# A hybrid attention block on one core: where the rotary blocks stand in the queues, and where the head norms stand in TensorE's order

## The chip, the cores and the metric

The kernel runs on one core of one Trainium2 chip. The metric is the device time of one execution in microseconds (us), lower is better; the times below are medians over runs of the same program. A core has TensorE (matmuls; PE in the profile, PEld for its weight loads), VectorE (DVE), ScalarE (ACT), GpSimd (POOL) and SyncE (SP), which in this kernel issues all DMA transfers. Every engine takes its instructions from its own queue in order; an instruction that waits holds up all that stand behind it on the same engine.

## The reference

The input is x, 512 positions by 2048 features, float32. One layer:

- h = RMSNorm(x) times a gain; one projection of h with `w_in` (2048 x 10752) gives all columns: q, k, v and gate z of branch A, q, k, v and gate z of branch B, and two merge gates of 2048.
- Branch A is differential attention with 8 heads: q and k get a rotary embedding, two softmaxes p1 - lambda p2 are applied to v, and the result of each head is RMS-normalised over its 128 features.
- Branch B has 8 query heads and 2 key/value heads. Each head's q and k are RMS-normalised over 128 features, multiplied by a gain, and rotated by a 2-D ("axial") rotary embedding; then softmax attention.
- Each branch's result times SiLU(z) goes through its own output projection (1024 x 2048); the two are merged with sigmoid gates, projected once more (`w_o`, 2048 x 2048), added to x, and normalised with a final gain.

## The kernel before

All matmuls are done in a split form: a float32 matrix becomes a high part (a rounded copy, `w_hi`, made by ScalarE, line 111) and a low part (the rest, `w_lo`, made by VectorE, line 112), and each product is the sum of three matmuls. So a weight tile passes SP (load), ScalarE (high part), VectorE (low part) and then TensorE. Three buffers hold the split tiles (`wp`, line 90), so the splitting engines run at most a little ahead of TensorE.

Most of the projection is done in Strassen groups (`strassen`, line 193, and `strassen_wide`): a block of 512 columns is made from seven products, a11, a12, s1, s2, s3, s4 and a22, instead of eight. The sums and differences of the weight blocks that Strassen needs are further VectorE work (`sub`, line 214; "L216" in the profile). Each product is 48 matmuls over two weight tiles. When results are complete the group calls `done`, which adds (VectorE) and stores.

The work in order:

1. x is normalised and transposed; the first columns, one plain Strassen group and two wide groups give branch B's and part of branch A's columns, which go to the DRAM buffer `pv`, one block of 128 columns each.
2. Twelve Strassen groups make the gates za, zb, ga, gb (lines 636 to 650). `gate` adds the last product (line 641), applies SiLU or sigmoid on ScalarE (line 642) and stores (line 644). After each of the first ten groups the program text calls `rope_b(n)`, which handles one of branch B's ten blocks (8 query, 2 key): it reads the block from `pv` into a tile `cols` (line 595, two buffers), takes four sums of squares on ScalarE (line 599), turns them into factors on POOL (`rsqrt_pool`, lines 107 and 108), makes the rotary products on VectorE (two half products, line 610, then lines 611 and 612), for key blocks multiplies by the factor on ScalarE (line 615), and stores the block back to `pv` (line 616).
3. The attention stage (from line 940). TensorE's order is written out by hand there (`manual_schedule`): sixteen heads of both branches, in the order of `HEADS`, are woven with "filler" steps, pieces of the remaining projections of 12 or 24 matmuls. `fill(n)` issues n filler steps; `FILLS` holds three digits per head, f[0] to f[2], used at three places of the head's turn. In head n's turn `last.finish()` ends the previous head, and `last.norm()` does the RMS norm of the previous head if it was of branch A (lines 809 to 824; two matmuls with a matrix of 1/128, then Ln, Exp and Square on ScalarE, three operations on VectorE, one on POOL, and the split of the result, `og0h` and `og0l`, or its store). For a B head `norm` does nothing.
4. Output projections, merge, final projection with Strassen groups, residual and final norm.

Outside the hand-written part a planner sets the order of each engine's instructions: it goes through the program with modelled durations and puts an instruction into the queue when its inputs are ready by that model, earlier text first. So an instruction whose inputs are ready early can stand in the queue far ahead of its place in the text. `tc.keep_in_program_order(ins)` adds an order edge: `ins` stands behind the instruction that was traced just before it on the same engine. It adds no wait on the chip by itself.

Of the kernel before, what the change touches and what calls it, by code (L numbers as in the profile page):

```python
# [13 lines left out]
AF = mybir.ActivationFunctionType  # L14
ALU = mybir.AluOpType
# [36 lines left out]
def hybrid_block_kernel(  # L52
# [8 lines left out]
    nc = tc.nc  # L61
# [7 lines left out]
    def new_banks(unit):  # L69
        ps_pools.close()  # L70
        banks["pool"] = unit, ps_pools.enter_context(
            tc.tile_pool(name="ps_" + unit, bufs=1, space=bass.MemoryType.PSUM))

    def share_banks(**kw):
        banks.update(kw)
# [29 lines left out]
    def rsqrt_pool(dst, ss, mul, add, n):  # L105

        nc.gpsimd.tensor_scalar(out=dst, in0=ss, scalar1=mul, scalar2=add, op0=ALU.mult, op1=ALU.add)
        nc.gpsimd.tensor_tensor(out=dst, in0=dst, in1=neg_half[:, :n], op=ALU.pow)
# [322 lines left out]
    with tc.tile_pool(name="xs", bufs=1) as xs:  # L431
# [4 lines left out]
        sq = xs.tile([P, D], F32, name="sq", tag="s4h")  # L436
        with tc.tile_pool(name="xn", bufs=1) as xn:
# [16 lines left out]
            for t in range(NT):  # L454
                ss = xn.tile([P, 2], F32, name="ss", tag="ss", bufs=4)
# [6 lines left out]
                for c in (slice(0, 512), slice(512, 1024)):  # L462
                    v = xt[:, t].rearrange("p (k c) -> p k c", k=2)[:, :, c]
# [95 lines left out]
        with tc.tile_pool(name="sp", bufs=6) as sp:  # L559
            new_banks("bank")  # L560
            free = [2 * i + j for i in banks["acc"] for j in range(2)]
            share_banks(acc=free[:4])

            def tmp():
                return sp.tile([P, 2, 256], F32, name="kept", tag="kept")

            for blocks in STRASSEN_BLOCKS[1:]:
                project(blocks, tmp, lambda ps: tmp())

            tabs = {}  # L570

            def b_table(nm, src):

                g = sp.tile([P, P], F32, name="g_" + nm, tag="g_" + nm, bufs=1)
                nc.sync.dma_start(out=g, in_=src.broadcast_to([P, P]))
                tcb = sp.tile([P, NT, P], F32, name=f"tc_{nm}", tag=f"tc_{nm}", bufs=1)
                tsb = sp.tile([P, NT, P], F32, name=f"ts_{nm}", tag=f"ts_{nm}", bufs=1)
                nc.sync.dma_start(out=tcb, in_=cos_b.rearrange("(t p) c -> p t c", p=P))
                nc.sync.dma_start(out=tsb, in_=sin_b.rearrange("(t p) c -> p t c", p=P))
                gv = g.rearrange("p (h r j) -> p h r j", h=2, r=2)  # L580
                for t in range(NT):
                    nc.gpsimd.tensor_tensor(out=tcb[:, t, :], in0=tcb[:, t, :], in1=g, op=ALU.mult)
                    ov = tsb[:, t, :].rearrange("p (h r j) -> p h r j", h=2, r=2)
                    for r in range(2):
                        nc.gpsimd.tensor_tensor(out=ov[:, :, r, :], in0=ov[:, :, r, :],
                                                in1=gv[:, :, 1 - r, :], op=ALU.mult)
                tabs[nm] = tcb, tsb

            def rope_b(n):


                b = B_QB + n if n < 8 else B_KB + n - 8
                assert written[b] == NT
                v = sp.tile([P, NT, P], F32, name="cols", tag="cols", bufs=2)
                nc.sync.dma_start(out=v, in_=pv[b])
                sq = sp.tile([P, P], F32, name="bsq", tag="bsq", bufs=1)
                ss = rb[:, n, :]
                for t in range(NT):
                    nc.scalar.activation(out=sq, in_=v[:, t, :], func=AF.Square, accum_out=ss[:, t:t + 1])
                if n < 8:  # L600

                    rsqrt_pool(ss, ss, 1.0, P * EPS, NT)
                else:
                    rsqrt_pool(ss, ss, 1.0 / P, EPS, NT)
                t2 = sp.tile([P, NT, P], F32, name="rope2", tag="rope2", bufs=1)
                tcb, tsb = tabs["q" if n < 8 else "k"]
                for r in range(2):
                    d, s, m = (x.rearrange("p t (a r j) -> p t a r j", r=2, j=32)[:, :, :, q, :]
                               for x, q in ((t2, r), (v, 1 - r), (tsb, r)))
                    nc.vector.tensor_tensor(out=d, in0=s, in1=m, op=ALU.mult)  # L610
                nc.vector.tensor_tensor(out=v, in0=v, in1=tcb, op=ALU.mult)
                nc.vector.tensor_tensor(out=v, in0=v, in1=t2, op=ALU.add)
                if n >= 8:
                    for t in range(NT):
                        nc.scalar.mul(out=v[:, t, :], in_=v[:, t, :], mul=ss[:, t:t + 1])
                nc.sync.dma_start(out=pv[b], in_=v)

            b_table("q", q_norm_g)
            b_table("k", k_norm_g)
            to_rope = [0, 8, 1, 2, 3, 4, 5, 9, 6, 7]  # L620


            nc.sync.dma_start(out=sub_g, in_=subln_g.rearrange("o p -> p o"))
            nc.vector.tensor_scalar(out=sub_g, in0=sub_g, scalar1=LAM_INIT - 1.0, scalar2=None, op0=ALU.mult)
            lam4, lprod = (sp.tile([P, n, 64], F32, name="lam", tag="kept") for n in (4, 2))
            for i, v in enumerate((lq1, lk1, lq2, lk2)):
                nc.sync.dma_start(out=lam4[:, i, :], in_=v.broadcast_to([P, 64]))
            for i in range(2):
                nc.vector.tensor_tensor(out=lprod[:, i, :], in0=lam4[:, 2 * i, :], in1=lam4[:, 2 * i + 1, :], op=ALU.mult)
            nc.vector.tensor_reduce(out=lsum, in_=lprod, axis=AX.X, op=ALU.add)  # L630
            nc.scalar.activation(out=lsum, in_=lsum, func=AF.Exp)
            nc.vector.tensor_tensor(out=nlam, in0=lsum[:, 1:2], in1=lsum[:, 0:1], op=ALU.subtract)
            nc.vector.tensor_scalar(out=nlam, in0=nlam, scalar1=-LAM_INIT, scalar2=None, op0=ALU.add)


            for c0, n, func, dst in ((O_ZA, BW, AF.Silu, zg[0:BW]), (O_ZB, BW, AF.Silu, zg[BW:]),
                                     (O_GA, D, AF.Sigmoid, gg[0:D]), (O_GB, D, AF.Sigmoid, gg[D:])):
                for g in range(0, n, S):
                    def gate(th, ch, ps, sb, g=g, func=func, dst=dst):
                        v = tmp()  # L640
                        nc.vector.tensor_tensor(out=v, in0=ps, in1=sb, op=ALU.add)
                        nc.scalar.activation(out=v, in_=v, func=func)
                        row = g + ch * 256
                        nc.sync.dma_start(
                            out=dst[row:row + 256, th * 256:th * 256 + 256].rearrange("(c p) t -> p c t", p=P),
                            in_=v)

                    strassen(w_in, c0 + g, c0 + g + 256, xq, False, tmp, gate)
                    if to_rope:
                        rope_b(to_rope.pop(0))  # L650
# [284 lines left out]
    def fill(n):  # L935
        for _ in range(n):
            next(filler, None)


    with tc.manual_schedule(engines={mybir.EngineType.PE}):  # L940
        heads = [(HeadA if h[0] == "A" else HeadB)(int(h[1])) for h in HEADS]
        heads[0].prepare()
        heads[1].prepare()
        heads[0].double()
        fill(FILL_FIRST)
        heads[0].turn()
        fill(2)
        for n, head in enumerate(heads):
            f = [int(c) for c in FILLS[n]]
            last = heads[n - 1] if n else None  # L950
            if n + 1 < len(heads):
                heads[n + 1].double()
            head.scores(0)
            head.scores(1)
            fill(f[0])
            if last:
                last.finish()
            head.scores(2)
            head.scores(3)
            if n + 1 < len(heads):  # L960
                heads[n + 1].turn()
            if n + 2 < len(heads):
                heads[n + 2].prepare()
            fill(1)
            if last:
                last.norm()
            fill(f[1] - 1)
            head.turn_p()
            fill(f[2])
        head.finish()  # L970
        head.norm()
# [11 lines left out]
    for n, e in (("s3", "h"), ("s4", "l")):  # L983
        m = xa.tile([P, 2, 8, 256], F32R, name="m" + n, tag="a2" + e)
        mq[n] = m[:, 0], m[:, 1]
    with tc.tile_pool(name="ya", bufs=1) as yp:
# [5 lines left out]
        for n in range(4):  # L992
# [15 lines left out]
            s = yp.tile([P, 2, 256], F32, name="ms", tag="ms")  # L1008
# [196 lines left out]
```

## Time and profile before

| | us |
|---|---|
| median of three timed runs | 1376.71 |
| lowest and highest of them | 1376.68, 1381.0 |
| the profiled execution, its own time | 1378.97 |
| its span in the trace | 1377.2 |
| TensorE busy | 1341.6 (97%) |
| VectorE busy | 1083.4 (79%) |
| ScalarE busy | 707.6 (51%) |
| POOL busy | 168.0 (12%) |

How to read it: the span is the time from the first to the last instruction of one execution; busy times are shares of it. Matmuls overlap each other, so a busy TensorE isn't TensorE at its best, and progress is better read from how many matmuls start in a stretch. The gates' stage lies from about 265 to 760 us of the span, the attention stage from 760 to about 1120 us.

### The profile page before, as it was taken

The page shows a single profiled execution, that of the slowest core. Times are in us where ns is not written, and L with a number is a line of the kernel's source. Part 1 is how long each engine was busy: PE and PEld are TensorE (multiplying, and loading weights), DVE is VectorE, ACT ScalarE, POOL GpSimd, SP SyncE. Part 2 cuts the span into 40 slices and gives each one's busy share as a digit, 9 for nine tenths or more (in the row PEclk, how much of TensorE's full clock was granted, in tenths as well). Part 3 has the DMA queues.
Part 4 walks back from the last instruction along what each step waited for, and adds up shares of the span by engine and source line. Part 5 has one row for each costly group of instructions (what it writes and reads, how often), then busy time and mean ns, then how long its engine had stood idle before and what let it go on. Part 6 is the DMA issues. An engine that isn't in the chain of part 4 may idle for free.

```text
span 1377.2 us, 22754 instructions
## 1 busy us (share of the span) xinstructions
PE 1341.6 (97%) x8905; PEld 1234.5 (90%) x8905; DVE 1083.4 (79%) x1339; ACT 707.6 (51%) x1119; POOL 168.0 (12%) x154
## 2 busy tenths in 40 slices
PE   6999999999999999999999999999899999999997
PEld 6998888899899999999999888888688888899997
DVE  5976978789887777778776477877899958899886
ACT  7643333355544444444444476666777843354444
POOL 1000000063100000000000321330321000004322
PEclk9999999999999999999999999999999999999999
DMA  8244663575444543343455774554765446463333
GB/s 290 77 144 134 190 200 99 170 213 167 138 129 141 153 145 118 117 125 118 146 154 146 229 220 132 153 153 133 209 179 168 147 152 203 148 245 117 95 97 123
DMA packets 198893, 214.12 MB, mean 155 GB/s; under 512 B 11760, under 2 KB 159488, under 8 KB 198144
## 3 DMA queue, kind: packets, MB, share of 16 engines
q1 hardware_dynamic: 198784, 212.65, 49.7%
q8 instruction: 70, 1.15, 0.4%
q14 instruction: 39, 0.32, 0.1%
HBM read 172.76 MB, written 35.65 MB: 151 GB/s over the span
## 4 chain that ended last, share of the span: by engine, by line
PE 62%; DVE 7%; DMA 3%; ACT 3%; issue 3%; POOL 1%; SPq 0%; DVEq 0%; POOLq 0%; ACTq 0%
PE acc L241 36%; PE acc L182 19%; PE aux L744 3%; DVE w_lo L112 2%; PE aux L731 2%; PE aux L857 1%; DMA pv<-cols 1%; DVE w_raw L216 1%; DMA cols<-pv 1%; PE aux L787 1%; PE aux L788 1%; ACT w_hi L111 1%; DVE nmax L699 1%; DMA rows<-yg 0%; DVE pl L112 0%
## 5 line engine op out<-in xcount | busy, mean ns | idle before, releaser
L111 ACT CAST w_hi<-w_raw 128x1024 fp32r<-128x1024 f32 x357 | 374.3, 1050 | 481.4 <-PE acc L241 291.6
L112 DVE TENSOR_TENSOR w_lo<-w_raw,w_hi 128x1024 fp32r<-128x1024 f32 x357 | 445.3, 1250 | 166.2 <-ACT w_hi L111 164.8
L216 DVE TENSOR_TENSOR w_raw<-w_raw 128x1024 f32<-128x1024 f32 x136 | 171.0, 1258 | 1.8
L241 PE MATMUL acc<-a2h,w_lo 128*128 128x256 f32 x384 | 109.1, 284 | 1.9 <-DVE w_lo L112 1.9
L241 PE MATMUL acc<-a2h,w_hi 128*128 128x256 f32 x384 | 108.9, 284 | 0.0
L241 PE MATMUL acc<-a2l,w_hi 128*128 128x256 f32 x384 | 108.8, 283 | 0.0
L687 POOL TENSOR_TENSOR cols<-cols,ca 128x512 f32<-128x512 f32 x16 | 21.5, 1341 | 537.1 <-DMA other<-pv 412.1
L241 PEld LDWEIGHTS acc<-a2h,w_lo 128*128 128x128 f32 x384 | 73.8, 192 | 2.5 <-DVE w_lo L112 2.5
L241 PEld LDWEIGHTS acc<-a2h,w_hi 128*128 128x128 f32 x384 | 73.8, 192 | 0.3 <-ACT w_hi L111 0.3
L241 PEld LDWEIGHTS acc<-a2l,w_hi 128*128 128x128 f32 x384 | 73.8, 192 | 0.0
L699 DVE TENSOR_REDUCE nmax<-aux 128x1 f32<-128x512 f32 x96 | 61.5, 682 | 2.8 <-PE aux L788 2.8
L182 PE MATMUL acc<-a1h,w_hi 128*128 128x512 f32 (+1 forms) x160 | 57.6, 364 | 0.2 <-ACT a1h L485 0.2
L182 PE MATMUL acc<-a1h,w_lo 128*128 128x512 f32 (+1 forms) x160 | 56.9, 360 | 0.0
L182 PE MATMUL acc<-a1l,w_hi 128*128 128x512 f32 (+1 forms) x160 | 56.7, 360 | 0.1
L241 PE MATMUL acc<-s2h,w_lo 128*128 128x256 f32 x192 | 54.8, 286 | 2.0 <-DVE w_lo L112 2.0
L241 PE MATMUL acc<-a1h,w_hi 128*128 128x256 f32 x192 | 54.6, 284 | 1.8 <-DVE wide_u L330 1.6
L241 PE MATMUL acc<-s4h,w_lo 128*128 128x256 f32 x192 | 54.6, 285 | 1.1 <-DVE w_lo L112 1.1
L182 PE MATMUL acc<-a2h,w_hi 128*128 128x512 f32 (+1 forms) x160 | 55.6, 351 | 0.0
L182 PE MATMUL acc<-a2l,w_hi 128*128 128x512 f32 (+1 forms) x160 | 55.6, 348 | 0.0
L182 PE MATMUL acc<-a2h,w_lo 128*128 128x512 f32 (+1 forms) x160 | 55.4, 347 | 0.0
L241 PE MATMUL acc<-a1h,w_lo 128*128 128x256 f32 x192 | 54.6, 284 | 0.8 <-DVE w_lo L112 0.8
L241 PE MATMUL acc<-s1h,w_lo 128*128 128x256 f32 x192 | 54.5, 284 | 0.2 <-DVE w_lo L112 0.2
(353 smaller groups left out, 4218.0 us busy)
## 6 DMA issues: line engine op xcount, KB each, us to landing
w_raw<-in_w_in_dram SPq DMA_DIRECT2D x144, 512.0 KB, 3.9
w_raw<-in_w_in_dram SPq DMA_DIRECT2D x64, 256.0 KB, 4.0
w_raw<-in_w_o_dram SPq DMA_DIRECT2D x32, 512.0 KB, 4.0
cols<-pv SPq DMA_DIRECT2D x36, 256.0 KB, 3.5
gg<-kept SPq DMA_DIRECT2D x32, 256.0 KB, 2.5
w_raw<-in_w_out_b_dram SPq DMA_DIRECT2D x32, 256.0 KB, 3.8
rows<-gg SPq DMA_DIRECT2D x32, 256.0 KB, 3.4
w_raw<-in_w_out_a_dram SPq DMA_DIRECT2D x32, 256.0 KB, 3.3
```

The source lines that it names most:

```text
L111: nc.scalar.copy(out=hi, in_=src)
L112: nc.vector.tensor_tensor(out=lo, in0=src, in1=hi.bitcast(F32), op=ALU.subtract)
L182: nc.tensor.matmul(out=acc[b][:, place], lhsT=l, rhs=r, start=first and kc == order[0] and k == 0 and i == 0, stop=last and kc == order[-1 ...
L216: nc.vector.tensor_tensor(out=d, in0=u, in1=v, op=ALU.subtract)
L241: nc.tensor.matmul(out=ps[u] if by_row else ps[:, u, :], lhsT=l, rhs=r, start=n % (2 if by_row else 4) == 0 and k == 0 and i == 0, stop=n ...
L687: nc.gpsimd.tensor_tensor(out=v, in0=v, in1=ca, op=ALU.mult)
L699: nc.vector.tensor_reduce(out=nmax, in_=sps, axis=AX.X, op=ALU.max, negate=True)
L731: nc.tensor.transpose(out=tp[:, i * P:(i + 1) * P], in_=self.p[i][:, j * P:(j + 1) * P], identity=ident)
L744: nc.tensor.matmul(out=o, lhsT=l, rhs=r, start=j == 0 and i == 0, stop=j == NT - 1 and i == 2)
L787: nc.tensor.matmul(out=sp, lhsT=qs[:, sl], rhs=kh, start=True, stop=False)
L788: nc.tensor.matmul(out=sp, lhsT=qs[:, sl], rhs=kl, start=False, stop=True)
L857: nc.tensor.matmul(out=sp, lhsT=l, rhs=r, start=n == 0, stop=n == 2)
```

## The change

Two things are changed. In `rope_b`, the four squares on ScalarE and the two half products on VectorE are each kept behind the instruction traced before them on their engine: the first of them behind the last result of the Strassen group that the text has just before, the others behind each other. In the heads' loop, the previous head's norm changes place with filler steps: it stood behind one filler step and ahead of f[1] - 1 of them, and now stands behind f[1] - 1 and ahead of one.

```diff
                 for t in range(NT):
-                    nc.scalar.activation(out=sq, in_=v[:, t, :], func=AF.Square, accum_out=ss[:, t:t + 1])
+                    tc.keep_in_program_order(
+                        nc.scalar.activation(out=sq, in_=v[:, t, :], func=AF.Square, accum_out=ss[:, t:t + 1]))
...
-                    nc.vector.tensor_tensor(out=d, in0=s, in1=m, op=ALU.mult)
+                    tc.keep_in_program_order(nc.vector.tensor_tensor(out=d, in0=s, in1=m, op=ALU.mult))
...
-            fill(1)
+            fill(f[1] - 1)
             if last:
                 last.norm()
-            fill(f[1] - 1)
+            fill(1)
             head.turn_p()
```

## Rows read from the trace of the kernel before

**Rows 1.** The page, part 1: busy us, share of the span, instructions.
```profile
PE 1341.6 (97%) x8905; PEld 1234.5 (90%) x8905; DVE 1083.4 (79%) x1339; ACT 707.6 (51%) x1119; POOL 168.0 (12%) x154
```

**Rows 2.** Busy time of two equal stretches: stretch, length, each engine, clock, DMA.
```profile
283.00:374.00 91.00, 84.63 (x678) 81.84 (x677) 81.40 (x104) 52.52 (x127) 31.05 (x32) 1.00 0.55 171
374.00:465.00 91.00, 91.00 (x760) 91.00 (x759) 68.85 (x66) 39.70 (x43) 0.00 (x0) 1.00 0.46 143
```

**Rows 3.** The same columns (PE, PEld, DVE, ACT, POOL), operations on `cols` alone.
```profile
283.00:374.00 91.00, 0.00 (x0) 0.00 (x0) 22.05 (x40) 17.43 (x84) 0.00 (x0) 1.00 0.55 171
```

**Rows 4.** Waits, 283 to 374 us: who waited for whom, us, times, longest.
```profile
ACT bsq L599 <- DMA cols<-pv: 16.2, 7, 4.7
PEld acc L241 <- DVE w_lo L112: 8.1, 10, 1.3
DVE rope L610 <- DMA cols<-pv: 4.6, 3, 1.8
ACT cols L615 <- POOL rb L108: 3.5, 1, 3.5
```

**Rows 5.** Timeline of VectorE: start, us, what, count [idle before it, releaser].
```profile
298.38 0.76 DVE L610 TENSOR_TENSOR rope<-cols,ts_q 128x256 f32<-128x256 f32 x2 [1.72 <-DMA cols<-pv]
299.06 1.22 DVE L112 TENSOR_TENSOR w_lo<-w_raw,w_hi 128x1024 fp32r<-128x1024 f32 x1
```

**Rows 6.** Timeline of VectorE and TensorE around 280 to 287 us.
```profile
280.09 0.23 DVE L629 TENSOR_TENSOR lam<-lam 128x64 f32<-128x64 f32 x1 [2.47 <-DMA lam<-in_lambda_k_dram]
...
286.89 0.39 PE L241 MATMUL acc<-s2h,w_lo 128*128 128x256 f32 x1 [0.57 <-DVE w_lo L112]
```

**Rows 7.** Timelines of VectorE, ScalarE and weight loads at a group's end.
```profile
437.04 0.68 DVE L641 TENSOR_TENSOR kept<-acc,kept 128x512 f32<-128x512 f32 x1
...
438.77 1.22 DVE L112 TENSOR_TENSOR w_lo<-w_raw,w_hi 128x1024 fp32r<-128x1024 f32 x1
...
437.88 0.62 ACT L642 ACTIVATE kept<-kept 128x512 f32<-128x512 f32 x1
439.81 1.05 ACT L111 CAST w_hi<-w_raw 128x1024 fp32r<-128x1024 f32 x1 [1.30 <-issue]
...
442.68 0.19 PEld L241 LDWEIGHTS acc<-a2h,w_lo 128*128 128x128 f32 x1
```

**Rows 8.** Waits of SP's queue, 260 to 380 us, then 380 to 760 us.
```profile
SPq L595 <- DMA pv<-cols: 15.2, 8, 3.9
...
SPq L644 <- ACT kept L642: 188.1, 38, 12.5
```

**Rows 9.** Operations on `cols`: ns min/median/max, first and last start; POOL's timeline.
```profile
L610 DVE TENSOR_TENSOR rope<-cols,ts_q x16: 418/422/543, 286.8 to 364.4; 128x256 f32<-128x256 f32 x16
...
328.39 3.45 POOL L107 TENSOR_SCALAR rb<-rb 128x4 f32<-128x4 f32 x1 [6.70 <-ACT bsq L599]
```

**Rows 10.** Timeline of TensorE at the norm of head A1.
```profile
897.72 0.50 PE L813 MATMUL aux<-sql,ones 128*128 128x512 f32 x1 [0.88 <-DVE sql L112]
```

**Rows 11.** TensorE at the norm of head A2, and the stretch behind it.
```profile
973.48 0.50 PE L812 MATMUL aux<-sqh,ones 128*128 128x512 f32 x1 [0.96 <-ACT sqh L111]
976.29 0.80 PE L813 MATMUL aux<-sql,ones 128*128 128x512 f32 x1 [2.32 <-DVE sql L112]
...
977.00:982.00 5.00, 5.00 (x14) 3.81 (x13) 2.43 (x6) 3.22 (x8) 0.00 (x0) 0.52 0.89 256
```

**Rows 12.** Norms of A3 and A4: timelines, waits from 1000 to 1116 us, busy time.
```profile
1024.33 0.39 PE L812 MATMUL aux<-sqh,ones 128*128 128x512 f32 x1
...
1028.22 0.69 ACT L815 ACTIVATE y<-aux,eps_t 128x512 f32<-128x512 f32 x1
...
1039.09 0.62 ACT L111 CAST og0h<-rows 128x512 fp32r<-128x512 f32 x1 [3.07 <-POOL rows L823]
...
ACT og0h L111 <- POOL rows L823: 6.6, 4, 3.1
...
1040.00:1056.00 16.00, 15.91 (x70) 12.48 (x69) 15.68 (x31) 14.48 (x31) 0.00 (x0) 1.00 0.46 137
```

## The prediction

> **What bounds the kernel now.** I read the page first. TensorE is busy 1341.6 us of 1377.2 [rows 1], so only its gaps and slow stretches, some 35 us with the start and the end, can be won back, and any idle time of another engine counts only where it ends in one. The second view is the busy time by stretch. The two stretches of 91 us in [rows 2] are the same code from about the same place of a Strassen group of the gates, once of the first group and once of the third. In 374 to 465 us TensorE starts 760 matmuls and never idles: one each 91/760 = 0.120 us. In 283 to 374 us it starts 678, so 82 x 0.120 = 9.8 us went. VectorE is busy 81.4 us of 91 in that stretch against 68.9 us, and 22.05 us of the 81.4 are operations on `cols`, the rotary blocks [rows 3]. All ten blocks lie here, the half products between 286.8 and 364.4 us [rows 9]; later stretches have none. The third view is the waits of the stretch [rows 4]: weight loads wait 8.1 us, ten times, for `w_lo`, the low half of the weight split, which VectorE makes; and VectorE and ScalarE themselves stand 4.6 and 16.2 us at a rotary block whose read from DRAM has not landed. [rows 5] shows one case: VectorE idles 1.72 us for `cols`, does the two half products, and only then makes, at 299.06 us, the `w_lo` for which a weight load stands (the longest of those ten waits, 1.3 us). Both engines take their instructions in order, so a block that is early in the queue and late in its data stops the weight split behind it.
>
> **The rotary blocks.** Nothing is removed or added: 40 squares on ScalarE, 20 half products and 20 full products and sums on VectorE, 20 small POOL operations and the rest stay. What changes is their place. The first square and the first half product of block n are ordered behind the last SiLU/sigmoid and the last add of group n; the others follow by data or by the chained edges. So the blocks go from ten in 91 us to one per group, and a group is 336 matmuls x 0.120 = 40.3 us.
>
> *What goes.* The 9.8 us, less what the blocks didn't cause. Just before, VectorE stood 2.47 us for the lambda vectors, and the `w_lo` that came behind them made TensorE wait 0.57 us at 286.89 us [rows 6]. The stretch lost 9.8 us of starts for 91 - 84.63 = 6.4 us of idle time, because the matmuls behind a gap start slower, so a gap costs 1.54 times its length: 0.9 us stay. Gain 9.8 - 0.9 = 8.9 us. The two reads that are issued at the start land long before their group ends; the other eight follow the store of the block two before, so they have about a group (40 us) where now they have none. The 4.6 and 16.2 us of waits go, and nothing of that kind is late next.
>
> *What a block costs in its new place.* On VectorE 22.05/10 = 2.2 us in one piece behind the last add; on ScalarE 17.43/10 = 1.75 us [rows 3], four squares with their accumulator reads. [rows 7] is such a place in the steady part: the add at 437.04 us, a subtraction, then the split that ends at 438.77 + 1.22 = 439.99 us, whose weights TensorE loads at 442.68 us. The lead is 2.7 us. With 2.2 us put behind the add, 0.5 us is left; the next ScalarE cast starts at 439.81 us, and the squares (from 438.5 us, 1.75 us long) delay it by 0.4 us, which the 2.2 us on VectorE hide. The two products that follow, a11 and a12, need no subtraction, so VectorE makes a split in 1.22 us for each tile of 24 matmuls, 2.88 us, and recovers 1.6 us a tile. I take 0 per group. If the lead were as short as inside 283 to 374 us, each block would cost its whole 2.2 us (22 us in ten groups); if the planner uses the room better, nothing is gained beyond the 9.8 us. The place read at 437 us is nearest, hence 0, with up to 0.6 us a group (6 us) kept for the range. The two key blocks also hold ScalarE for four multiplications that wait for POOL, 3.5 us in the one case seen [rows 4]; against the 2.7 us lead that is at most 0.8 us each, 1.6 us for the range.
>
> *Queues.* SP gets a store and a read per block; the read waits for a store to land, 15.2 us in eight, at most 3.9 [rows 8]. In the steady part SP stands 188.1 of 380 us for gate results, up to 12.5 us at a time [rows 8], so the block's store and read fit into such a pause: cost 0. If that cover were gone, the weight loads queued behind would start up to 3.9 us later in each of eight groups; how much of it TensorE would see I can't read, at most 31 us, at least 0, and the pauses put it at 0. POOL is empty from 374 to 760 us [rows 2], and nobody waits for its query factors before the heads.
>
> A rule speaks against the bursts. Row first: while POOL's little factor operation on 128x4 ran beside VectorE's two-input products, it took up to 3.45 us, but the half products had a median of 0.422 us and a longest of 0.543, against a shortest of 0.418 [rows 9]: POOL paid, hardly VectorE. The Trainium skill, GPSIMD Engine Reference, section 1 Specifications, says that POOL's SBUF interfaces are shared with VectorE, with contention for VectorE instructions that have two SBUF inputs; every operation of the burst is one. If VectorE paid, a burst could double to 4.4 us and pass the lead by 1.7 us, 17 us in ten groups; by this trace's row the sum stays.
>
> **The norms.** `fill(1)` and `fill(f[1] - 1)` swap places around `last.norm()`. Norm work exists only after an A head. With a middle digit of 2 (the heads after A0 and A2) both are 1 and nothing moves. It moves for A1 and A3 to A6, by one filler step, 12 matmuls x 0.227 = 2.7 us later; A7's stands outside the loop. A1's second norm matmul waits 0.88 us for `sql` [rows 10]; 2.7 us later `sql` is there, so 0.9 us go. A3 to A6 had practically no wait (TensorE is busy 15.91 of 16 us around A4's [rows 12]): 0 to 0.4 us, I take 0. The norm's chain (Ln, Exp, Square, three on VectorE, the product on POOL) starts up to 2.7 us later; its tiles are next needed by the `finish` of the A head behind, nearly a whole head later. A2's stall, the largest of the attention part, stays: 0.96 and 2.32 us of waits, and then 5 us at a granted clock of 0.52, the 1.2 GHz level for nearly all of that stretch, which is 5 x 0.48 = 2.4 us lost [rows 11].
>
> **Sum.** -8.9 (blocks) + 0 (bursts) - 0.9 (A1) + 0 (other norms) = -9.8 us. The profiled execution took 1378.97 us (1377.2 us of span and 1.8 around it), so it would be 1369.2 us. Against the median of the three timed runs, 1376.71 us, which is 2.3 us lower, it is 1366.9 us; I say 1367.
>
> **Rivals.**
> *A: the bursts cost.* The order in VectorE's queue is planned with modelled durations; if the burst falls beside two subtractions instead of one, the lead of 2.7 us is passed by about 0.6 us a group. 6 us come back, with the key blocks up to 7: 1373 us. For it: VectorE is 76% busy in the steady part already (68.85 of 91 us, [rows 2]). Against: [rows 7], and the recovery in a11 and a12.
> *B: A2's stall goes too.* The other engines' instructions are planned anew, and the 3.3 us of waits and the 2.4 us of slow clock may vanish: 1361 us. For it: it is a matter of queue order on ScalarE and VectorE. Against: its norm isn't moved.
> *C, slower: the later norms stop ScalarE.* For A3 to A6 the cast `og0h` of the finished head stands in ScalarE's queue ahead of the next head's exponentials and waits for POOL's product: 3.07 us at A3, 6.6 us in four [rows 12]. If that product comes the full 2.7 us later and the cast keeps its place, ScalarE loses 2.7 us per head, and VectorE, busy 15.68 of 16 us there [rows 12], can't make it up: 4 x 2.7 = 10.9 us. With waits of that length the clock can fall as at A2, 4 x 2.4 = 9.6 us more: 1366.9 + 20.5 = 1387 us. It decides once the cast's wait exceeds what TensorE has queued; at 3.07 us TensorE idled 0.1 us there, so from about 3 us on. Against: A3's norm matmul starts at 1024.33 us and its Ln only at 1028.22 [rows 12], held by ScalarE's queue, so a later matmul needn't make a later Ln. The Trainium skill, TensorE: Matmul & The Clock Gate, part 1, says that the clock follows how busy the array has recently been, and A2's rows agree (granted 0.52 behind 3.3 us of waits).
> *D: no effect.* The edges bind only to the instruction traced just before on that engine. If those weren't the group's last results, the blocks would stay early and only A1 would gain: 1375.6 us. Against: in the code the last traced ScalarE and VectorE instructions are those of the last `done`.
>
> **From this to the numbers.** Forecast 0.62; A 0.14; B 0.10; C 0.09; D 0.05. The forecast's own range is 1363 to 1371. B opens the lower side, to 1360.5; A and part of D the upper side, to 1375.5, and that leaves out C, the rest of D and a little of B, less than 0.2. 0.3% (4.1 us) is about what a measurement of this kernel can tell from no change: faster is then below 1372.6 us. Forecast, B and nearly half of A make 0.79 faster; the rest of A, D and a little of C 0.13 same; 0.08 slower.
>
> **What would show it.** In the trace after, the squares and half products lie one block per 40 us, from about 306 to 670 us; the stretch 283 to 374 us has over 745 matmuls; waits of weight loads for `w_lo` in the gates are about 1 us in total; stretches behind stay at 758 or more per 91 us (if they fall, A). A1's `sql` wait is gone and A2's stands. I am wrong if the gates' stage is not about 9 us shorter, or if TensorE waits by more than 3 us in the heads behind A3.

## The result and the profile after

The kernel after takes 1368.45 us (median of 4 runs, 1367.33 to 1369.72) against 1377.48 us of the kernel before in the same session: ratio 0.993, interval 0.991 to 0.995. The forecast was 1367.0. The profiled execution took 1369.72 us with a span of 1367.5, so its own difference is 9.3 us (9.7 of span). From about line 600 on, a line of the kernel after has a number one higher than the same line before.

Page, part 1 (answers to [rows 1]): TensorE has 3.8 us less busy time for the same 8905 matmuls, and VectorE has 3 us more in a shorter span.

```profile
PE 1337.8 (98%) x8905; PEld 1232.9 (90%) x8905; DVE 1086.4 (79%) x1339; ACT 709.5 (52%) x1119; POOL 166.9 (12%) x154
```

Busy time by stretch, the two of [rows 2] and one more: stretch, length, PE, PEld, DVE, ACT, POOL with their counts, granted clock, DMA share, GB/s.

```profile
283.00:374.00 91.00, 90.41 (x753) 90.08 (x751) 73.38 (x78) 45.70 (x66) 11.68 (x16) 1.00 0.50 154
374.00:465.00 91.00, 91.00 (x761) 91.00 (x760) 71.58 (x74) 43.56 (x61) 3.70 (x4) 1.00 0.50 154
465.00:556.00 91.00, 91.00 (x761) 91.00 (x760) 74.92 (x78) 44.18 (x68) 5.56 (x6) 1.00 0.43 135
```

(A count takes in the matmuls under way at the edges of a stretch, in every such row alike.) The first stretch has 753 matmuls, not 678, and VectorE is 73.4 us busy there, not 81.4; the later stretches carry the blocks now (71.6 us where it was 68.9) and still have 761. The eight that the first stretch lacks lie ahead of 290 us, behind the lambda vectors. From there on, before and then after:

```profile
290.00:374.00 84.00, 78.21 (x628) 75.76 (x628) 74.43 (x93) 45.68 (x110) 24.05 (x23) 1.00 0.56 174
290.00:374.00 84.00, 84.00 (x703) 84.00 (x701) 66.94 (x69) 40.47 (x60) 4.68 (x8) 1.00 0.50 155
```

Where the blocks lie, in the operations on `cols` (count: ns min/median/max, first and last start), against [rows 9]:

```profile
L600 ACT ACTIVATE bsq<-cols x40: 292/311/312, 308.5 to 672.7; 128x128 f32<-128x128 f32 x40
L611 DVE TENSOR_TENSOR rope<-cols,ts_q x16: 411/415/417, 307.8 to 671.0; 128x256 f32<-128x256 f32 x16
```

The waits of the first stretch that are left on TensorE, against 8.1 us, ten times, in [rows 4]; VectorE and ScalarE no longer wait for a rotary block's read:

```profile
PEld acc L241 <- DVE w_lo L112: 0.8, 1, 0.8
PE acc L241 <- DVE w_lo L112: 0.6, 1, 0.6
```

The norms of A1 and then A2 in TensorE's timeline, against [rows 10] and [rows 11] (start, us, what, count, [idle before it, releaser]):

```profile
890.39 0.39 PE L813 MATMUL aux<-sqh,ones 128*128 128x512 f32 x1
890.63 0.40 PE L814 MATMUL aux<-sql,ones 128*128 128x512 f32 x1
...
964.20 0.50 PE L813 MATMUL aux<-sqh,ones 128*128 128x512 f32 x1 [1.23 <-ACT sqh L111]
966.96 0.79 PE L814 MATMUL aux<-sql,ones 128*128 128x512 f32 x1 [2.27 <-DVE sql L112]
```

A1's wait is gone. A2's pair starts 9.3 us earlier than before (964.20 against 973.48) and waits 3.50 us where it waited 3.28.

### The profile page after: what moved, and what is told of

The parts are those of the page before. It is cut to its first block, busy times and chain, and to the rows that moved or that the text cites. A ratio compares the mean times of both kernels' runs of the same rounds, so it can differ in the third digit from the quotient of the medians.

```text
span 1367.5 us, 22737 instructions
## 1 busy us (share of the span) xinstructions
PE 1337.8 (98%) x8905; PEld 1232.9 (90%) x8905; DVE 1086.4 (79%) x1339; ACT 709.5 (52%) x1119; POOL 166.9 (12%) x154
## 4 chain that ended last, share of the span: by engine, by line
PE 88%; DVE 5%; ACT 2%; DMA 2%; issue 2%; SPq 1%; POOL 0%; DVEq 0%; POOLq 0%; ACTq 0%
PE acc L241 45%; PE acc L182 23%; PE acc L322 11%; PE aux L745 3%; DVE w_lo L112 2%; PE aux L732 2%; PE aux L858 1%; PE aux L788 1%; PE aux L789 1%; DVE w_raw L216 1%; DMA xt<-in_x_dram 1%; ACT w_hi L111 0%; PE aux L481 0%; DMA lam<-in_lambda_k_dram 0%; DMA rows<-og 0%
## 5 line engine op out<-in xcount | busy, mean ns | idle before, releaser
L241 PE MATMUL acc<-s3l,w_hi 128*128 128x256 f32 x192 | 54.3, 283 | 0.0
L241 PE MATMUL acc<-s3h,w_lo 128*128 128x256 f32 x192 | 54.3, 283 | 0.0
L241 PE MATMUL acc<-a1l,w_hi 128*128 128x256 f32 x192 | 54.3, 283 | 0.0
```

Of the source, the lines that this page charges most:

```text
L241: nc.tensor.matmul(out=ps[u] if by_row else ps[:, u, :], lhsT=l, rhs=r, start=n % (2 if by_row else 4) == 0 and k == 0 and i == 0, stop=n ...
```

## The experiments

Every kernel below is a small edit of the kernel before or of the kernel after, as its expectation says. Its rows come from one profiled execution. Times are medians, ratios are to the kernel before in the same session (1377.2 to 1378.0 us).

**Blocks alone, norms alone.** The two parts of the change, each without the other.

> The rotary blocks are kept behind their groups; the norms stay where they were. Theory (the bunched blocks stopped the weight splits): the gates' stage ends 8.9 us earlier as in the changed kernel, A1's wait of 0.9 us stays, in all about 8 us less than before, 1369.4 us, about 1 us over the changed kernel. Rival (the norms' place gave the gain): within 1 us of before, 1377 us.

> Only the norms have their later place. Theory: A1's wait goes, 0.9 to 1 us less than before, 1376.5 us; no loss at A3 to A6; A2's stall stays. Rival (the norms gave the gain): 1369 us. Second rival (the later norms cost ScalarE up to 2.7 us a head at A3 to A6): 1380 us or more, and waits of TensorE between 1000 and 1116 us.

Measured: blocks alone 1369.75 us, ratio 0.9948 (0.9935 to 0.996); norms alone 1375.67 us, 0.9994 (0.9985 to 1.0003). The blocks are the whole measurable gain. With the norms alone A1's wait for `sql` goes as in the kernel after, but a gap of 0.48 us opens at 899.6 us, where the projection waits for ScalarE's copy of `kq`: the 0.9 us moved rather than left. Two things in the profile of blocks alone are not as expected. The lambda vectors land earlier there (VectorE stands 1.2 us for them, 2.4 us in the kernel after), so the gap behind them is gone and the first stretch has 761 matmuls. And A1's wait for `sql` is 1.71 us, not 0.9.

**One pin at a time.** A pin is here the order edge that `keep_in_program_order` adds.

```diff
-nc.scalar.activation(out=sq, in_=v[:, t, :], func=AF.Square, accum_out=ss[:, t:t + 1])
+tc.keep_in_program_order(nc.scalar.activation(...))      # act only
...
-nc.vector.tensor_tensor(out=d, in0=s, in1=m, op=ALU.mult)
+tc.keep_in_program_order(nc.vector.tensor_tensor(...))   # dve only
```

> Only VectorE's half products are kept behind the group; the squares on ScalarE are free; norms as before. The products that follow depend on the half products, so a block's VectorE work and its store are spread anyway. If VectorE's crowding was the cause, the gates' stage gains the whole 8.9 us: 1368.6 us. If the late reads in ScalarE's queue were a part of it, each of eight blocks still stops ScalarE for up to 4.7 us at its read, against a lead of 2.7 us: up to 2 us per block come back, 1369 to 1377 us, and the weight splits wait for ScalarE behind `cols`.

> Only ScalarE's squares are kept behind the group; the half products are free; norms as before. The full product overwrites the tile that the squares read, so VectorE's second half of a block waits for them and the blocks are spread anyway. Theory (crowding in the stretch): the gates' stage gains about 8.9 us, 1368.6 us, less what the half products still lose at late reads: at most 1.8 us each, under the lead, so under 1 us in all. Rival (both pins are needed, as the free half products and what they hold back stop VectorE): less than half the gain, over 1373 us.

Measured: VectorE's pin alone 1369.0 us, 0.9945 (0.9932 to 0.9957); ScalarE's alone 1369.64 us, 0.9953 (0.994 to 0.9967). Either one spreads the blocks: with ScalarE's the half products lie from 287.0 to 637.9 us, with VectorE's the squares from 281.2 to 603.4 us. With VectorE's pin ScalarE still stands 5.2 us, four times, for a late block read, and TensorE has 748 matmuls in the first stretch. All that are missing lie ahead of 290 us, behind the lambda vectors (VectorE stands 3.0 us for them); from 290 to 374 us there are 703, as in the kernel after. So late reads on ScalarE alone, with the blocks spread, cost nothing that shows.

**Earlier reads.** First four buffers instead of two for the blocks, nothing else.

```diff
-v = sp.tile([P, NT, P], F32, name="cols", tag="cols", bufs=2)
+v = sp.tile([P, NT, P], F32, name="cols", tag="cols", bufs=4)
```

> The kernel before with four buffers instead of two for the blocks' tile, nothing else: more reads are issued ahead, the blocks stay bunched at the front of the gates. It parts two causes of the 9.8 us: reads that are late in the queue, and too much VectorE work in one stretch. If late reads are the cause, VectorE's 4.6 us and ScalarE's 16.2 us of waits shrink to under a third and the gates' stage gains 5 us or more: 1369 to 1372 us. If the amount of work is the cause (22 us of blocks on top of 69 us fill the 91 us wholly), the blocks bunch more tightly and the stage gains at most 2 us or loses some: 1375 to 1380 us.

Measured: 1376.4 us, 0.9986 (0.9977 to 0.9996), 681 matmuls in the first stretch. The edit did only half of what it was for: VectorE's wait for block reads went, ScalarE's stayed, since the last six reads still follow a store.

```profile
ACT bsq L599 <- DMA cols<-pv: 14.6, 6, 4.5
...
PEld acc L241 <- DVE w_lo L112: 5.3, 8, 1.1
```

So this run could not say whether late reads or the crowd of blocks costs the time. The last run of the study did, with six buffers and without the store that the reads wait for:

```diff
-v = sp.tile([P, NT, P], F32, name="cols", tag="cols", bufs=2)
+v = sp.tile([P, NT, P], F32, name="cols", tag="cols", bufs=6)
...
-                nc.sync.dma_start(out=pv[b], in_=v)
```

> The kernel before (blocks not pinned), with six buffers for the rotary blocks and without the store of each finished block; no read then waits for a store, and all ten should land before their turn. The blocks' arithmetic stays, crowded into the first groups; what is left out is that branch B's attention reads the rotated and normalised q and k, so its output is not the reference's. It tells apart the two halves of my account of the 8.9 us. Theory of lateness: the loss comes of VectorE and ScalarE standing in order for reads that have not landed (4.6 and 16.2 us before). Then, without such waits, most of the gaps between 299 and 374 us go though the blocks stay crowded: over 740 matmuls in 283 to 374 us, time 1368 to 1371. Theory of crowding: ten blocks in two groups ask for more of VectorE than it has beside the splits (a rotary product or sum, a subtraction and a split are 0.68 + 1.22 + 1.22 = 3.1 us against 2.9 us of matmuls for each tile of weights): the waits for reads go, the w_lo waits of 0.4 to 1.3 us stay, below 700 matmuls, 1375 to 1377. A share of each, 1371 to 1375, would be read off the count of matmuls missing from 761.

Measured: 1370.96 us, 0.9952 (0.9939 to 0.9965). The blocks stay crowded (half products from 288.0 to 345.7 us). VectorE waits for none of their reads, ScalarE for one, 4.5 us, ahead of the first square at 283.44 us. Busy time by stretch, its first 91 us, then from 290 us on, then three pieces of 20 us:

```profile
283.00:374.00 91.00, 89.18 (x735) 88.21 (x734) 87.64 (x110) 57.12 (x133) 28.23 (x31) 1.00 0.50 157
290.00:374.00 84.00, 83.68 (x693) 83.11 (x692) 80.67 (x99) 50.74 (x116) 21.23 (x21) 1.00 0.50 154
...
303.00:323.00 20.00, 19.85 (x165) 19.89 (x166) 19.81 (x25) 15.22 (x42) 10.05 (x9) 1.00 0.36 116
323.00:343.00 20.00, 19.98 (x167) 19.78 (x166) 19.86 (x28) 8.42 (x12) 0.00 (x0) 1.00 0.56 171
343.00:363.00 20.00, 20.00 (x169) 20.00 (x169) 19.86 (x22) 9.93 (x12) 0.00 (x0) 1.00 0.31 93
```

VectorE is busy 59.5 of 60 us in those pieces and TensorE 59.8. From 290 us on it has 693 matmuls; the kernel after has 703 and the kernel before 628. So nearly all of that loss is gone. The rest of the 26 that are missing from 761 belongs to one gap of 1.35 us, whose `w_lo` stands behind the product of the lambda vectors:

```profile
282.87 0.48 DVE L628 TENSOR_TENSOR lam<-lam 128x64 f32<-128x64 f32 x1 [0.90 <-DMA lam<-in_lambda_k_dram]
283.28 1.49 DVE L112 TENSOR_TENSOR w_lo<-w_raw,w_hi 128x1024 fp32r<-128x1024 f32 x1
...
284.83 0.39 PE L241 MATMUL acc<-s2h,w_lo 128*128 128x256 f32 x1 [1.35 <-DVE w_lo L112]
```

(From 283 to 290 us there are 44 matmuls here and 61 in blocks alone, where that gap is absent.) The ten left, 1.2 us, are all that crowding can have cost from 290 us on, against 75 matmuls, 9.0 us, in the kernel before.

Three reservations. The count of 735 is under the 740 that the expectation asked for, because of that gap; the vectors land later here, with six block reads issued right behind them, and whether these delay them is not shown. The time by itself proves less than the count: matmul for matmul, this profile ends 9.4 us ahead of the kernel before, but only 6.6 us of it arise in the gates and 2.4 us at A2's norm. And without the stores SP's queue is lighter, and the planner's order is another (the last square starts at 313 us, not 361). In the kernel before, no engine waits for a weight's read between 283 and 374 us, so a lighter queue can hardly have helped but through the blocks' own reads.

**No blocks.** They are left out of the kernel before.

> The kernel before without the rotary blocks: the norm factors are a constant and branch B's q and k go to the heads as projected, so the reads, squares, products and stores of the blocks are left out. It measures what the spread blocks still cost. Theory (a burst behind each group costs TensorE nothing): the gates' stage is as long as in the changed kernel within 0.5 us, the time 1368 to 1370 us. Rival (each burst costs a little): 2 to 6 us under the changed kernel, 1362 to 1366 us, all of it between 283 and 680 us.

Measured: 1368.65 us, 0.9931 (0.9917 to 0.9946); 756 matmuls in the first stretch and 703 from 290 us on, as many as in the kernel after: in their new place the blocks cost TensorE nothing there. The time agrees: blocks alone, which has the same norms, takes 1.1 us more, and the intervals overlap.

**Two blocks per group.**

```diff
-                    if to_rope:
+                    for _ in to_rope[:2]:
                         rope_b(to_rope.pop(0))
```

> The kernel after, with two rotary blocks behind each of the first five groups instead of one behind each of ten. Theory: a block is hidden because its 2.2 us on VectorE is shorter than the 2.7 us between the last add of a group and the weight load that needs the next split. Then two blocks, 4.4 us, pass that by 1.7 us: a gap of about 1.7 us of weight loads behind w_lo at each of five groups, 8.5 us in all, time about 1377 (no better than before). Rival: the room is larger than the one place read (the planner puts splits between the parts of the blocks, and TensorE has more weights ready), so that two blocks still cost under 0.4 us a group: 1368.5 to 1370.5; then what hurt before was only that all ten came without any group between them. A third outcome, half of it, 1371 to 1374: the lead model holds, but part of the delay is made up in a11 and a12.

Measured: 1366.41 us (1365.99 to 1368.53), 0.9926 (0.9914 to 0.9939). The lead model falls. Busy time of two stretches, then waits of the first one:

```profile
283.00:374.00 91.00, 89.87 (x747) 89.46 (x746) 75.72 (x83) 47.08 (x81) 38.52 (x21) 1.00 0.52 164
374.00:465.00 91.00, 91.00 (x761) 91.00 (x760) 74.13 (x81) 48.54 (x81) 8.10 (x8) 1.00 0.51 164
```

```profile
ACT cols L616 <- POOL rb L108: 5.8, 1, 5.8
...
PEld acc L241 <- DVE w_lo L112: 1.0, 1, 1.0
PE acc L241 <- DVE w_lo L112: 0.8, 1, 0.8
PEld acc L241 <- ACT w_hi L111: 0.6, 1, 0.6
```

Four of five groups with two blocks lose nothing. The first loses 1.1 us of idle time (688 matmuls from 290 us on, where the kernel after has 703), and by another way: the key block's multiplications hold ScalarE 5.8 us for POOL's factor, and the casts `w_hi` behind them come late. POOL itself is slow there. Its factor operation (count: ns min/median/max, first and last start) is recorded at 9.29 us in that group, while VectorE goes from one operation to the next beside it:

```profile
L107 POOL TENSOR_SCALAR rb<-rb x10: 318/3389/9292, 309.4 to 482.8; 128x4 f32<-128x4 f32 x10
```

That it is faster than the kernel after by 2 us is at the edge of what these runs can tell; its profile ends 0.8 us ahead, and that is at A2's norm and behind the lambda vectors, whose gap is absent here, not at the blocks.

**The norm still later.** By the whole filler, and then behind the turn of `p`.

```diff
-            fill(f[1] - 1)
-            if last:
-                last.norm()
-            fill(1)
+            fill(f[1])
+            if last:
+                last.norm()
             head.turn_p()
```

> The changed kernel with the norm behind all of the middle filler steps, so one step later still: this moves A0's and A2's norms too, by 12 matmuls, 2.7 us. Theory (A2's norm matmuls stand in TensorE's order ahead of a late sql, and the 1.2 GHz stretch follows from that wait): of 1.23 + 2.27 us of waits at most 0.8 us stay, the granted clock stays at the 2.4 GHz level, gain 2.7 to 3.5 us plus 2.4 us of clock: 1363 us. Rival (ScalarE and VectorE are the limit there, so the wait moves to the next matmul that needs them): TensorE waits as long at the scores or at the turn of p behind, 1367 to 1369 us.

```diff
-            fill(f[1] - 1)
-            if last:
-                last.norm()
-            fill(1)
+            fill(f[1])
             head.turn_p()
+            if last:
+                last.norm()
             fill(f[2])
```

> As the one before, but with the norm behind the turning of p too (16 transposes, 1.75 us more): 4.5 us later than in the changed kernel at A2. Theory: A2's waits are gone wholly and the clock stays up, 1362 to 1363 us, if the norm's chain for A3 to A6 still ends before the next head needs its tiles. Rival (the later chain stops ScalarE at og0h for A3 to A6, 2 us or more per head): 1366 to 1372 us, with new waits of TensorE between 1000 and 1110 us.

Measured: 1374.94 us (0.9976, 0.9964 to 0.9988) and 1374.64 us (0.9978, 0.9967 to 0.9989): 6 us of the gain are lost again. TensorE's waits from 760 to 1116 us (us, times, longest), in the first and then the second; the kernel after has 4.4 us there, all but 0.9 of it at A2's norm:

```profile
PE aux L858 <- DVE y L821: 3.4, 2, 2.2
PE acc L182 <- DVE rows L921: 2.3, 2, 1.3
PE aux L788 <- DVE y L821: 2.2, 1, 2.2
PE aux L732 <- DVE p L696: 1.5, 2, 0.9
```

```profile
PE aux L732 <- DVE p L696: 2.5, 2, 1.7
PE acc L182 <- DVE rows L921: 2.4, 2, 1.8
PE acc L182 <- ACT og1h L111: 2.3, 1, 2.3
```

In the first, the score matmuls (L858, L788) stand until VectorE's first norm operation (L821) has read the norm's sum out of its `aux` bank; a norm that is issued later gives the bank back later. In the second, the turn of `p` waits for its scaling (L696) and the projections for their operands.

**The two gaps that were left.** The lambda block behind the gates, and four buffers for the rows read back from `og`.

```diff
-            nc.sync.dma_start(out=sub_g, in_=subln_g.rearrange("o p -> p o"))
-            ...
             for c0, n, func, dst in (...):
                 ...
+            nc.sync.dma_start(out=sub_g, in_=subln_g.rearrange("o p -> p o"))
+            ...
```

> The kernel after, with the lambda and subln_g loads and their seven small operations moved behind the gates. Theory: the 0.6 us weight-load wait near 287 us was VectorE standing at the lambda vectors' DMA (2.5 us), the one gap left in the gates, worth 0.9 us with the slower starts behind it: the stretch 283 to 374 us then has 758 or more matmuls, time 1367.5, a difference that can hardly be told from none. Rival: the gap comes from the end of the projections before (the split of the first group is late in any case), and stays: 751 to 753 matmuls. A third: in their new place at the stage's end the small operations hold the first attention head instead, 1 to 3 us slower, 1369.5 to 1371.5.

```diff
-                hi_lo(*og_act(k), load_rows(og, k, "og", 2))
+                hi_lo(*og_act(k), load_rows(og, k, "og", 4))
```

> The kernel after, with four buffers instead of two for the rows read back from og (the finished heads' outputs), so that these reads are issued earlier. Theory: A2's sql and sqh waits (1.2 and 2.3 us), and the 5 us at a granted clock near half behind them, come of ScalarE's and VectorE's og1 casts, which stand in both queues with their reads late (5.8 us of ScalarE waits in 940 to 1000 us): these waits go to under 1 us, A2's stall under 1 us, time 1363 to 1366. Rival: as in the two kernels whose norms are later, A2's relief is given back within 30 us, since VectorE is over 95% busy there and what TensorE waits for next is its order, not the reads: 1368 to 1369. A third: the reads issued earlier push the other SP loads (kq, cols, weights) back: 1370 to 1373.

Measured: lambda later 1369.19 us (0.9938, 0.9924 to 0.9952), no better in time (a new gap of 0.75 us at 792 us takes most of it back), but the row is as expected, without a gap behind the lambda vectors. Blocks alone has such a row too, with the lambda block in its old place, so this one doesn't show that the move did it.

```profile
283.00:374.00 91.00, 91.00 (x761) 91.00 (x760) 71.04 (x73) 43.16 (x62) 12.76 (x22) 1.00 0.48 151
```

More `og` buffers 1369.18 us (0.9946, 0.9933 to 0.9958): the rival holds. ScalarE's waits for `og` reads halve (5.8 to 2.8 us in 940 to 1000 us), but A2's two waits shrink only from 3.5 to 2.8 us, and a gap of 1.16 us opens at 890 us, behind ScalarE's copy of `kq`.

```profile
ACT og1h L111 <- DMA rows<-og: 2.8, 2, 2.0
...
PE aux L813 <- ACT sqh L111: 1.6, 1, 1.6
...
PE aux L814 <- DVE sql L112: 1.2, 1, 1.2
```

## Why the prediction was right, step by step

*Blocks, -8.9.* Right in size, with some luck. Matmul for matmul, the one that ended the last of the old stalls starts at 364.76 us instead of 373.58: -8.8. The residual that was left standing, 0.9 us behind the lambda vectors, is there too: 0.59 us of idle time in the kernel after, eight matmuls short of 761. But it comes of this execution rather than of the kernel, for it depends on when the lambda vectors land. Five kernels have these same gates (the kernel after, blocks alone, the two later norms, more `og` buffers). VectorE stood 2.4 us for the vectors in the first of them and 1.2 to 1.6 us in the others, which have 759 to 761 matmuls; in blocks alone the gates end 10.0 us ahead of the kernel before. The cause was named as an engine that stands in order behind a late read; that was shown only by the last run, in which ten crowded blocks with reads on time cost 1.2 us at most from 290 us on. The sentence on VectorE's load (81.4 us against 68.9) was no part of the cause: it can be 59.5 of 60 us busy while TensorE is busy 59.8.

*Bursts, 0.* Right in size, wrong in its picture. There is no burst of 2.2 us in one piece. VectorE's timeline behind the group's last add, in the place of [rows 7]:

```profile
428.12 0.68 DVE L642 TENSOR_TENSOR kept<-acc,kept 128x512 f32<-128x512 f32 x1
428.72 0.75 DVE L611 TENSOR_TENSOR rope<-cols,ts_q 128x256 f32<-128x256 f32 x2
429.39 1.22 DVE L112 TENSOR_TENSOR w_lo<-w_raw,w_hi 128x1024 fp32r<-128x1024 f32 x1
430.52 1.22 DVE L216 TENSOR_TENSOR w_raw<-w_raw 128x1024 f32<-128x1024 f32 x1
431.66 0.68 DVE L612 TENSOR_TENSOR cols<-cols,tc_q 128x512 f32<-128x512 f32 x1
432.26 1.21 DVE L112 TENSOR_TENSOR w_lo<-w_raw,w_hi 128x1024 fp32r<-128x1024 f32 x1
433.39 0.68 DVE L613 TENSOR_TENSOR cols<-cols,rope 128x512 f32<-128x512 f32 x1
```

Only the half products are held behind the add. The full product and the sum are free, and stand one at a time between the splits, so no piece of the block holds a split back by more than about 0.7 us. The first split even starts 1.27 us behind the start of the add here and 1.73 us in [rows 7], because a subtraction stood ahead of it there. The lead of 2.7 us against 2.2 us therefore decided nothing, and rival A, which set a burst against that lead, had no ground: two blocks per group would have passed it by 1.7 us and lost nothing in four groups of five.

*Queues, 0.* Right. From 380 to 760 us ScalarE waits for some weight reads, which it doesn't in the kernel before, and TensorE still has 761 matmuls per 91 us:

```profile
ACT w_hi L111 <- DMA w_raw<-in_w_in_dram: 7.3, 4, 1.8
```

*The rule against the bursts.* In the kernel after no half product runs beside POOL's factors; all ten full products do, and take 0.679 to 0.683 us, as the sums do that run alone (0.678 to 0.682). So VectorE paid nothing. POOL is where the crowding showed: its factor operation took 0.192 to 3.447 us in the kernel before, is even now, and takes up to 9.29 us with two blocks per group.

```profile
L107 POOL TENSOR_SCALAR rb<-rb x10: 517/522/524, 310.3 to 673.2; 128x4 f32<-128x4 f32 x10
```

The Trainium skill, GPSIMD Engine Reference, section 1 Specifications, has VectorE's two-input instructions contend with POOL; for operations of POOL this small, the measurement has the loss on POOL's side alone. For a large one it can fall on VectorE: A1's `sql` in the kernel before took 1.26 us beside a POOL product of 128x512, and about 0.68 us at every other head, so 0.6 us of that split, most of the wait of 0.88 us in [rows 10], came with POOL's product. In the kernel after the two met again, and POOL paid: its product took 2.28 us and `sql` 0.67. Both rows in the kernel before:

```profile
896.40 1.26 DVE L112 TENSOR_TENSOR sql<-osq,sqh 128x512 fp32r<-128x512 f32 x1
...
895.83 1.28 POOL L686 TENSOR_TENSOR other<-other,sa 128x512 f32<-128x512 f32 x1 [1.97 <-DMA other<-pv]
```

*Norms, -0.9.* Right at its place: the matmul behind A1's norm is 9.9 us ahead (890.86 us against 900.79), 1.0 more than the gates give. At A2 it is 9.3, since the wait for `sqh` there grew by 0.27 us and the one for `sql` did not shrink. But the experiments give the move no value in time that can be told: alone it measures 0.9994, and blocks alone and the kernel after have overlapping intervals. Nor was 0.9 a fixed price. With the norm in its old place A1's wait is 0.88 us in the kernel before, 1.71 with blocks alone, 1.77 with VectorE's pin, and none with ScalarE's.

*Rivals.* C saw its mechanism start: from 1000 to 1116 us ScalarE's cast stands 10.2 us for POOL's product, five times, against 6.6 us in [rows 12].

```profile
ACT og0h L111 <- POOL rows L824: 10.2, 5, 3.1
```

The longest is still 3.1 us, at the point from which it was to decide, and TensorE loses 0.35 us in all there, at other work. One step of the filler later (the first of the two later norms) the loss was real, and 5.6 us of the waits were for the `aux` bank, at A0 to A2. From 1000 us on that cast stands up to 4.0 us there and TensorE waits 2.5 us for other work; whether the cast lies behind that is not shown. B did not come, but its ground holds: with VectorE's pin alone A2's waits are 1.06 and 1.20 us, though its norm is not moved. D is refuted by where the blocks lie (its time, by its own terms, would be 1376.7 - 0.9 = 1375.8 us). Sum measured at the last matmul: -9.6 us, forecast -9.8.

## What to carry to other kernels

When an engine takes its instructions in order, ask of each side job in its queue when its data lands, before asking how busy the engine is: here reads that came up to 4.7 us late, bunched behind each other's stores, cost 9 us, and the same arithmetic with the reads on time, VectorE 99% busy, cost about one. To spread such jobs, tying one instruction of each to a point of the main work is enough: either pin alone spread the blocks, and the free rest filled in between the splits. What it costs to tie the rest too was not tried. A consumer that is moved later also gives back its buffer later; look at who waits for that bank before moving it.

## What was not expected of the hardware

TensorE's clock behind two waits did not follow their sum. Stretches just behind A2's norm, first in the blocks-alone kernel (waits of 0.53 and 2.19 us), then with two blocks per group (1.12 and 1.13 us), then in the kernel after (1.23 and 2.27 us):

```profile
965.00:970.00 5.00, 3.44 (x17) 2.87 (x18) 4.49 (x11) 4.51 (x10) 0.00 (x0) 1.00 0.90 278
```

```profile
967.00:969.50 2.50, 2.50 (x6) 2.02 (x7) 2.46 (x6) 2.50 (x6) 0.00 (x0) 0.50 1.04 292
```

```profile
967.00:969.50 2.50, 2.50 (x6) 2.02 (x7) 2.03 (x6) 2.50 (x6) 0.00 (x0) 0.50 0.92 262
969.50:972.00 2.50, 2.50 (x7) 1.92 (x7) 0.86 (x2) 1.44 (x3) 0.00 (x0) 0.50 0.82 258
```

2.7 us of waiting left the clock at 2.4 GHz in the first (it fell later, to a mean of 0.66 in 975 to 980 us, behind three more waits of 0.31 to 0.59 us), and 2.3 us halved it in the second. Why is open; no run here tries it.
